# Hybrid mLSTM/attention encoder layer: the output projection's stores move from SP's queue to POOL's

## The chip, the cores and the metric

The kernel runs as one launch on one core of a Trainium2 chip. The metric is device time in microseconds (us), the median of several runs. The core's engines work through their own instruction queues, each in order: TensorE (PE, with a separate queue PEld for weight loads), VectorE (DVE), ScalarE (ACT), GpSimd (POOL) and SyncE (SP). Engines wait for one another through semaphores. A transfer (DMA) is issued by an instruction in the queue of one of the engines, and then runs by itself; in this kernel SP and POOL issue them.

## The reference

The reference is one encoder layer, in float32, over two groups of tokens with the same weights: 2048 prompt tokens and 256 sample tokens, 2304 in all, of width 1024.

```python
# per layer: x += W_out [ mLSTM_heads(n) ; GQA_heads(n) ],  n = RMSNorm(x)
#            x += W_down( silu(g) * a ),  [a; g] = DWConv3(W_up RMSNorm(x))
# final RMSNorm
D_MODEL = 1024; SEQ = 2048; DEC_SEQ = 256; D_FF = 2816
M_HEADS = 8; A_HEADS = 8; A_KV_HEADS = 2; HEAD_DIM = 64
```

A combined input projection feeds eight bidirectional mLSTM heads and eight query heads of attention, whose outputs are concatenated ("mix", width 1024). The output projection W_out brings mix back to the model's width and adds it to x; call the sum x1. A second RMSNorm of x1, call it n2, goes into the FFN: up projection, a width-3 depthwise convolution along the tokens, a gate, and the down projection, which is added to x1.

## The kernel before

Every float32 product is made on PE as three products of a shorter type, after a split of each operand into a high part (ACT) and the remainder, the low part (DVE). The phases are: input projections and norms; gates; then attention and mLSTM, interleaved; then the output projection, called phase_c, which starts while attention still has some query blocks to do and runs mixed with it; then the FFN, whose first loads and sums are mixed with the end of phase_c. All intermediate tensors go through DRAM: mix_d (the concatenated head outputs), x1_d (residual sums), n2_d (normalised rows), n2t_d (sums of n2 that a Strassen-like scheme for the up projection uses).

phase_c loads its weights first and splits them, and then goes through nine blocks of 256 tokens. For block b:

- `loads(b)`: eight loads from mix_d into the tiles cmx (L988), each split by ACT (L989) and DVE (L990), and eight loads of x into the four tiles cx{b}_0 to cx{b}_3 (L994). There are eight buffers for cx, so block b + 2 reuses those of block b.
- `mm(b, z)`: for each of four quarters z of the output columns, 48 matmuls into po (L1003); 9 × 4 × 48 = 1728 in all.
- `post(b, z)`: DVE adds po to cx in place (L1008); the sum is stored to x1_d (L1009, 128 partitions by 512 numbers, 256 KB); ACT squares it (L1011); POOL adds the squares up (L1013).
- `tail(b)`, called after the first quarter of the next block: POOL folds the sum of squares (L1016); a helper makes the reciprocal root mean square and broadcasts it to all partitions (PE L128, DVE L131, POOL L132, PE L134, tile rs_c); DVE multiplies cx in place by it and by the norm's weight, eight instructions (L1020); each quarter is stored to n2_d (L1022, 256 KB).

Before the change both stores go through `g.st`, which is `nc.sync`: SP's queue. POOL's own transfers near by are attention's stores into mix_d (L622), and earlier in the kernel the loads of k and v and, in mLSTM, those of dm (L821).

Attention, per block of queries: score products px and their maximum on DVE (L557, L558), a transpose of the maximum m4r (L566, PE L569 into pr), scores again (L580, L581), exponentials on ACT (L584, L585), the low part on DVE (pl, L586), products with v into pv (L598). At the end of a block ACT copies the sums out of pv (L606 the values, L607 the row sums), DVE takes reciprocals (L615, four instructions), POOL multiplies (L619) and issues two stores into mix_d (L622). Block b of phase_c can only start when the mix rows of its tokens are there; for the last block these come from attention's last query block.

The FFN's start: `n2_load` reads n2_d and n2t_d and splits (L1069 to L1071, tiles n and nt); `n2_sums` makes the sums (L1086 to L1092); `up_start` loads two slabs of the up weights (L1102, L1103, tiles ru), makes four weight sums on POOL (L1124 to L1127, tiles tw, one of them written over ru), splits (ACT L1115, DVE L1116) and multiplies into pa, pb, pc (L1119). The results go through ACT (L1135, L1206), the convolution on DVE (L1213) and the gate (L1287 to L1299). The down weights are loaded into rd (L1302), split into wd (ACT L1308, DVE L1309) and used at L1257; DVE adds into acc (L1259), which is first loaded from x1_d (L1189). The tiles ru, rd and rn share one pool of four buffers.

The order of instructions in each engine's queue is not the order of the program text. The framework simulates the timeline while it builds the program and puts out the instructions in the order in which they become ready in that simulation; attention's instructions have a higher priority. So an edit of one instruction's engine can change the order around it on all engines.

Of the kernel before, what the change touches and what calls it, by code (L numbers as in the profile page):

```python
# [36 lines left out]
BT = 256  # L37
# [48 lines left out]
def f32(ap):  # L86
    return ap.bitcast(F32)
# [14 lines left out]
def split(g, hi, lo, src, r, col=None):  # L102
    nc = g.nc
    nc.sync.dma_start(r, src)
    nc.scalar.activation(hi, r, AF.Copy, scale=1.0 if col is None else col)
    if col is None:
        nc.vector.tensor_tensor(lo, r, f32(hi), ALU.subtract)
    else:
        nc.vector.scalar_tensor_tensor(lo, r, col, f32(hi), ALU.mult, ALU.subtract)
# [10 lines left out]
def rstd_bc(g, sp, pp, sqs, n, ptag, name, bufs=1):  # L120


    nc = g.nc
    k = n // P
    ps = pp.tile([P, 512], F32, tag=ptag, name="rs_" + name, bufs=bufs)
    for t in range(k):
        for i, sq in enumerate(sqs):
            nc.tensor.matmul(ps[:, 504 + 2 * t:506 + 2 * t], sq[:, t * P:(t + 1) * P], g.ones, start=i == 0,  # L128
                             stop=i == len(sqs) - 1)
    r = sp.tile([P, 4], F32, tag="rcol", name="rcol_" + name)[:, 0:k]  # L130
    nc.vector.tensor_scalar(r, ps[:, 504:504 + 2 * k].rearrange("p (t o) -> p t o", o=2)[:, :, 0], EPS, None, ALU.add)  # L131
    nc.gpsimd.tensor_tensor(r, r, g.mhalf[:, 0:k], ALU.pow)  # L132
    for t in range(k):
        nc.tensor.matmul(ps[:, t * P:(t + 1) * P], r[:, t:t + 1].to_broadcast([P, P]), g.ident, start=True, stop=True)  # L134
    return ps[:, 0:n]
# [824 lines left out]
def phase_c(g, sn, sp, pp, wps):  # L960

    nc = g.nc
    wo = []
    g.normed = set()

    def weights(c):

        wo.append([wps[c // 4].tile([P, 2, 512], F32R, tag="w", name=f"wo{c}_{k}", bufs=WB) for k in range(2)])  # L970
        for k, w in enumerate(wo[c]):
            if c < 4:
                t = g.raw.tile([P, 512], F32, tag="raw", name=f"ro{c}_{k}", bufs=2)
            else:
                t = sp.tile([P, 512], F32, tag="x", name=f"ro{c}_{k}", bufs=CX)
            split(g, w[:, 0, :], w[:, 1, :], g.w_out[0, c * P:c * P + P, 512 * k:512 * k + 512], t)

    def loads(b):
        mx = []
        x = [sp.tile([P, 2, BT], F32, tag="x", name=f"cx{b}_{z}", bufs=CX) for z in range(4)]  # L980
        for z in range(4):
            for o in range(2):
                c = 2 * z + o
                if b % 2:
                    m = sp.tile([P, 2, BT], F32R, tag="mx", name=f"cmx{b}_{c}", bufs=MXB)
                else:
                    m = sn.tile([P, 2, BT], F32R, tag="nT", name=f"cmx{b}_{c}", bufs=NTB)
                nc.sync.dma_start(f32(m[:, 1]), g.mix_d[b, :, c])  # L988
                nc.scalar.activation(m[:, 0], f32(m[:, 1]), AF.Copy)  # L989
                nc.vector.tensor_tensor(m[:, 1], f32(m[:, 1]), f32(m[:, 0]), ALU.subtract)  # L990
                mx.append(m)
        for z in range(4):
            for t in range(2):
                nc.sync.dma_start(x[z][:, :, t * P:(t + 1) * P], g.xT[2 * b + t, :, 2 * z:2 * z + 2])  # L994
        return x, mx

    def mm(b, z, mx):
        po = pp.tile([P, 2, BT], F32, tag="po", name=f"po{b}_{z}")
        for o in range(2):
            n = slice(((2 * z + o) % 4) * P, ((2 * z + o) % 4 + 1) * P)  # L1000
            for c in range(NCC):
                for k, (a, h) in enumerate(((0, 0), (0, 1), (1, 0))):
                    nc.tensor.matmul(po[:, o], wo[c][z // 2][:, a, n], mx[c][:, h, :],  # L1003
                                     start=(c == 0 and k == 0), stop=(c == NCC - 1 and k == 2))
        return po

    def post(b, z, x, po, acc):
        nc.vector.tensor_tensor(x[z], po, x[z], ALU.add)  # L1008
        g.st.dma_start(g.x1_d[b, :, 2 * z:2 * z + 2], x[z])  # L1009
        q = acc if z == 0 else sp.tile([P, 2, BT], F32, tag="sq", name=f"csq{b}_{z}", bufs=1)  # L1010
        nc.scalar.activation(q, x[z], AF.Square, scale=1.0 / 32.0)  # L1011
        if z:
            nc.gpsimd.tensor_tensor(acc, acc, q, ALU.add)  # L1013

    def tail(b, x, acc):
        nc.gpsimd.tensor_tensor(acc[:, 0], acc[:, 0], acc[:, 1], ALU.add)  # L1016
        r = rstd_bc(g, sp, pp, [acc[:, 0]], BT, "r", f"c{b}")
        for z in range(4):
            for o in range(2):
                nc.vector.scalar_tensor_tensor(x[z][:, o], x[z][:, o], g.n2w[:, 2 * z + o:2 * z + o + 1],  # L1020
                                               r, ALU.mult, ALU.mult)
            g.st.dma_start(g.n2_d[:, 2 * z:2 * z + 2, b * BT:(b + 1) * BT], x[z])  # L1022
        g.normed.add(b)

    for c in range(NCC):
        weights(c)
        if c % WSTEP == WSTEP - 1:
            yield None
    prev = None
    for b in range(NB):  # L1030
        yield 2 * b
        x, mx = loads(b)
        for z in range(4):
            po = mm(b, z, mx)
            if z == 0:
                if prev is not None:
                    tail(*prev)
                acc = sp.tile([P, 2, BT], F32, tag="acc", name=f"cacc{b}", bufs=1)
            post(b, z, x, po, acc)
            if z < 3:  # L1040
                yield None
        prev = (b, x, acc)
    g.c_end = lambda: tail(*prev)


# [471 lines left out]
```

## Time and profile before

| | us |
|---|---|
| median of 3 runs | 3474.17 |
| lowest and highest | 3474.0, 3474.66 |
| the profiled execution's own time | 3475.05 |
| its span in the trace | 3473.3 |

The page of the profile lists 404.29 MB moved by DMA in 258,501 packets, 32.3% of the DMA engines' time for the transfers that SP and ACT issue ("hardware dynamic", q1) and 3.5% for those that POOL issues ("software dynamic", q0).

In a profile, L12 is line 12 of the kernel; "out<-in" are the names of tiles with buffer numbers left out. A row of the timeline gives the start, the length, the engine, the line and the operation, how many instructions were joined into the row ("x4"), and in brackets the idle time just before it and what released it. SPq and POOLq are the sequencers of SP and POOL: a DMA's issue is a row there, and the transfer itself a row "DMA". A row of the waits gives the engine and the line that waited, what it waited for, the total, the number of times and the longest.

### The profile page before, as it was taken

How to read it: one execution, taken by the hardware profiler on the slowest of the kernel's cores; microseconds unless marked ns; L12 is line 12 of the kernel's file. 1: busy time of each engine (PE TensorE's matmuls, PEld its weight loads, DVE VectorE, ACT ScalarE, POOL GpSimd, SP SyncE). 2: the span in 40 equal slices, each digit the busy share in tenths (PEclk: the TensorE clock that was granted, in tenths of full speed). 3: DMA queues.
4: the chain of work that ended last, by engine and by line, in shares of the span. 5: the costliest groups of instructions: out<-in, count | busy, mean ns of one | idle time of the engine just before them, and what ended most of it. 6: DMA issues, size and time to landing. Idle time of an engine off the chain costs nothing. (4 is left out here: it accounts for less than half of the span.)

```text
span 3473.3 us, 55765 instructions
## 1 busy us (share of the span) xinstructions
PE 3346.2 (96%) x20058; PEld 3103.0 (89%) x20058; DVE 2670.5 (77%) x4654; ACT 1930.9 (56%) x4329; POOL 1103.9 (32%) x1328
## 2 busy tenths in 40 slices
PE   7989999999999999999988999999999999999998
PEld 6878888888888887987778999999999998999998
DVE  6875687677777789767666888888888878887776
ACT  4536566666666766645554444446544446555555
POOL 6643133222224322211116233225333224322222
PEclk9999999999999999999999999999999999999999
DMA  6765334343355443432218233223333223421221
GB/s 222 238 197 162 117 107 118 104 131 101 105 169 161 131 144 115 145 105 70 68 51 296 73 97 98 74 65 130 127 105 99 67 73 119 145 65 63 73 73 50
DMA packets 258501, 404.29 MB, mean 116 GB/s; under 512 B 33552, under 2 KB 158256, under 8 KB 258224
## 3 DMA queue, kind: packets, MB, share of 16 engines
q1 hardware_dynamic: 230320, 358.24, 32.3%
q0 software_dynamic: 11344, 33.04, 3.5%
q10 hardware_dynamic: 16560, 9.44, 0.9%
q8 instruction: 158, 2.59, 0.3%
q14 instruction: 119, 0.97, 0.1%
HBM read 316.73 MB, written 83.90 MB: 115 GB/s over the span
## 5 line engine op out<-in xcount | busy, mean ns | idle before, releaser
L1257 PE MATMUL pd<-act,wd 128*128 128x384 f32 (+1 forms) x3120 | 593.2, 336 | 25.2 <-DVE acc L1259 14.4
L1257 PEld LDWEIGHTS pd<-act,wd 128*128 128x128 f32 x3120 | 539.5, 189 | 34.0 <-DVE acc L1259 20.0
L586 DVE TENSOR_TENSOR pl<-ps,ph 128x512 fp32r<-128x512 f32 x520 | 354.1, 685 | 235.3 <-ACT ps L585 228.2
L1119 PE MATMUL pa<-nt,wut 128*128 128x386 f32 (+2 forms) x2376 | 454.5, 339 | 2.0 <-DVE nt L1071 2.0
L1119 PEld LDWEIGHTS pa<-nt,wut 128*128 128x128 f32 x2376 | 421.4, 190 | 2.3 <-DVE nt L1071 2.3
L584 ACT ACTIVATE ph<-ps 128x512 fp32r<-128x512 f32 x520 | 309.7, 596 | 177.1 <-PE ps L581 172.3
L558 DVE TENSOR_REDUCE mx<-px 128x1 f32<-128x512 f32 (+1 forms) x528 | 343.8, 671 | 67.4 <-PE px L557 65.4
L1213 DVE SCALAR_TENSOR_TENSOR y<-u,cw,y 128x768 f32<-128x768 f32 (+1 forms) x264 | 314.0, 1190 | 36.3 <-ACT y L1206 29.2
L598 PE MATMUL pv<-ph,v 128*128 128x512 f32 (+1 forms) x1040 | 330.2, 405 | 2.9 <-ACT ph L584 2.4
L1124 POOL TENSOR_TENSOR tw<-ru 128x512 f32<-128x512 f32 x66 | 91.1, 1380 | 744.4 <-DMA ru<-w_up 573.3
L1135 ACT ACTIVATE u<-pa 128x386 f32<-128x386 f32 (+2 forms) x264 | 128.4, 486 | 328.4 <-PE pa L1119 326.9
L585 ACT ACTIVATE ps<-ps 128x512 f32<-128x512 f32 x520 | 310.9, 599 | 0.0
L1259 DVE TENSOR_TENSOR acc<-pd,acc 128x384 f32<-128x384 f32 (+1 forms) x544 | 280.6, 536 | 34.5 <-PE pd L1257 33.5
L1003 PEld LDWEIGHTS po<-cmx,wo 128*128 128x128 f32 x1728 | 233.9, 191 | 32.6 <-ACT cmx L989 16.2
L1003 PE MATMUL po<-cmx,wo 128*128 128x256 f32 x1728 | 242.2, 284 | 14.9 <-ACT cmx L989 14.8
L580 PE MATMUL ps<-qq,kk 128*128 128x512 f32 x520 | 217.0, 421 | 1.8 <-DVE pl L586 1.1
L557 PE MATMUL px<-kk,qq 128*128 128x512 f32 (+1 forms) x528 | 207.7, 411 | 6.6 <-DVE pl L586 3.5
L598 PE MATMUL pv<-pl,v 128*128 128x512 f32 x520 | 206.6, 407 | 6.9 <-DVE pl L586 6.6
L581 PE MATMUL ps<-qm,kl 65*128 65x512 f32 x520 | 209.1, 405 | 0.0
L724 PE MATMUL mj<-mn,wm 128*128 128x256 f32 x1296 | 197.4, 288 | 3.5 <-ACT og L738 2.1
L724 PEld LDWEIGHTS mj<-mn,wm 128*128 128x128 f32 x1296 | 182.1, 192 | 17.6 <-ACT og L738 2.5
L734 PE MATMUL mv<-wm,mn 128*128 128x256 f32 x1296 | 196.2, 288 | 1.1 <-ACT qb L730 0.9
(288 smaller groups left out, 7239.0 us busy)
## 6 DMA issues: line engine op xcount, KB each, us to landing
ru<-w_up SPq DMA_DIRECT2D x132, 512.0 KB, 3.4
mn<-n_d SPq DMA_DIRECT2D x216, 256.0 KB, 3.3
rd<-w_down SPq DMA_DIRECT2D x66, 512.0 KB, 3.6
n_d<-n1T SPq DMA_DIRECT2D x18, 1024.0 KB, 5.6
dm<-nm_d POOLq DMA_DIRECT2D x72, 256.0 KB, 4.0
mjn<-n_d SPq DMA_DIRECT2D x72, 256.0 KB, 3.3
mvn<-n_d SPq DMA_DIRECT2D x72, 256.0 KB, 3.2
q_d<-qz SPq DMA_DIRECT2D x18, 512.0 KB, 3.5
```

The lines of the kernel that those rows point to most:

```text
L558: nc.vector.tensor_reduce(s.mx[:, t, z0:z0 + 1], ps[:, 0:w], AX.X, ALU.max)
L580: nc.tensor.matmul(ps, kk[:, kc:kc + P], s.qq[:, 0:N], start=True, stop=False)
L584: nc.scalar.activation(ph, ps, AF.Exp)
L585: nc.scalar.activation(ps, ps, AF.Exp)
L586: nc.vector.tensor_tensor(pl, ps, f32(ph), ALU.subtract)
L598: nc.tensor.matmul(s.pv[0:HD if k in (1, 3) else P, 0:N], v, p, start=(kp == 0 and k == 0), stop=(2 * kp + 2 == s.nk and k == 5))
L724: nc.tensor.matmul(pj[:, o], s.w[c][:, a, o * P:(o + 1) * P], nT[c][:, :, h, :], start=(c + o + k == 0), stop=(c == NCC - 1 and k == 2 and ...
L1003: nc.tensor.matmul(po[:, o], wo[c][z // 2][:, a, n], mx[c][:, h, :], start=(c == 0 and k == 0), stop=(c == NCC - 1 and k == 2))
L1119: nc.tensor.matmul(p, w[:, aa, c, :], ops[k][:, c, bb, 0:n], start=c == 0 and i == 0 and not add, stop=c == NCC // 2 - 1 and i == 2, skip_ ...
L1213: nc.vector.scalar_tensor_tensor(y[:, s:e], u[:, s + k:e + k], cw[:, k, jj:jj + 1], y[:, s:e], ALU.mult, ALU.add)
L1257: nc.tensor.matmul(po, wds[j][c // 4][:, aa, c % 4 * P:(c % 4 + 1) * P], acts[j][:, bb, z0:z1], start=(j == 0 and k == 0), stop=(j == len( ...
L1259: nc.vector.tensor_tensor(accs[c][:, z0:z1], po, accs[c][:, z0:z1], ALU.add)
```

## The change

Two lines differ. In each, the issuing engine of a store is POOL instead of SP; the transfers are the same in source, target and size.

```diff
     def post(b, z, x, po, acc):
         nc.vector.tensor_tensor(x[z], po, x[z], ALU.add)
-        g.st.dma_start(g.x1_d[b, :, 2 * z:2 * z + 2], x[z])
+        nc.gpsimd.dma_start(g.x1_d[b, :, 2 * z:2 * z + 2], x[z])
...
                 nc.vector.scalar_tensor_tensor(x[z][:, o], x[z][:, o], g.n2w[:, 2 * z + o:2 * z + o + 1],
                                                r, ALU.mult, ALU.mult)
-            g.st.dma_start(g.n2_d[:, 2 * z:2 * z + 2, b * BT:(b + 1) * BT], x[z])
+            nc.gpsimd.dma_start(g.n2_d[:, 2 * z:2 * z + 2, b * BT:(b + 1) * BT], x[z])
```

They are executed 36 times each, nine blocks by four quarters. Other users of `g.st` keep SP.

## The prediction

> **What bounds the kernel now.** I read the page first: the span, busy shares, and the chain that ended last by engine.
>
> ```profile
> span 3473.3 us, 55765 instructions
> PE 3346.2 (96%) x20058; PEld 3103.0 (89%) x20058; DVE 2670.5 (77%) x4654; ACT 1930.9 (56%) x4329; POOL 1103.9 (32%) x1328
> PE 34%; DVE 7%; DMA 3%; issue 1%; ACT 1%; POOL 0%; SPq 0%; POOLq 0%; DVEq 0%; ACTq 0%
> ```
>
> PE is busy for 96% of the span. SP's and POOL's queues have 0% of the chain of waits, so an issue slot is not in itself what ends the program. PE's 127 us of idle time are spread over everything; the question is how much lies where the diff acts. The 72 stores fall between 1409.7 and 1892.0 us, so the second view is the table of windows over 1388 to 1912 us (columns: length, then busy time and count for PE, weight loads, DVE, ACT, POOL, then granted clock, DMA share, GB/s).
>
> ```profile
> ...
> 1560.00:1640.00 80.00, 73.66 (x402) 59.77 (x402) 53.92 (x93) 43.09 (x84) 11.09 (x13) 0.96 0.21 63
> 1640.00:1720.00 80.00, 74.60 (x409) 59.38 (x408) 55.73 (x96) 43.51 (x84) 10.16 (x11) 0.98 0.20 60
> 1720.00:1800.00 80.00, 74.63 (x384) 59.87 (x383) 54.24 (x94) 46.95 (x93) 8.08 (x9) 0.94 0.19 56
> ...
> 1815.00:1829.00 14.00, 0.08 (x1) 0.00 (x0) 6.40 (x13) 1.60 (x3) 2.39 (x3) 0.66 0.66 189
> 1829.00:1872.00 43.00, 42.98 (x346) 42.98 (x347) 20.89 (x29) 12.88 (x20) 32.12 (x30) 0.95 0.95 324
> 1872.00:1912.00 40.00, 36.02 (x198) 35.36 (x198) 34.03 (x43) 26.41 (x46) 24.07 (x15) 0.96 0.81 273
> sum 524.00, PE 488.00 PEld 424.67 DVE 354.80 ACT 276.47 POOL 123.22; mean PE 48.80 PEld 42.47 DVE 35.48 ACT 27.65 POOL 12.32
> ```
>
> In these 524 us PE is idle for 36: 17.1 in the three 80 us windows (6.34 + 5.40 + 5.37), 13.9 in the gap from 1815 to 1829, 4.0 after 1872, 1 elsewhere. That 36 us (1.0% of the span) caps any gain. The view of waits over 1380 to 1960 us says who ends them (total, times, longest).
>
> ```profile
> SPq L1009 <- DVE cx L1008: 94.4, 21, 11.6
> SPq L1022 <- DVE cx L1020: 65.8, 24, 16.5
> POOL o L619 <- DVE rs L615: 131.0, 9, 29.5
> ...
> PE po L1003 <- ACT cmx L989: 14.8, 3, 13.9
> PE pv L598 <- DVE pl L586: 6.5, 5, 1.8
> PE pr L569 <- DVE m4r L566: 6.0, 3, 4.1
> ```
>
> SP does stand behind the stores: 94.4 + 65.8 us of its queue is waiting for DVE's results, with loads behind. But PE's own waits are for DVE (attention's maximum m4r, its low half pl) and once, for 13.9 us, for cmx. None but the cmx wait ends in a load.
>
> **The change part by part.** It takes 36 stores of x1 (L1009) and 36 of n2 (L1022) off SP's queue and issues the same 72 transfers, 256 KB each, on POOL. Nothing is computed differently. What a slot costs on either queue is in the views by source line.
>
> ```profile
> L1009 SPq DMA_DIRECT2D x_d<-cx x36: 319/326/865, 1409.7 to 1874.9; - x36
> DMA to landing us min/median/max: 2.1/2.6/6.0
> L1022 SPq DMA_DIRECT2D n_d<-cx x36: 359/371/1139, 1459.4 to 1892.0; - x36
> L622 POOL DMA_DIRECT2D mix_d<-o x56: 532/577/714, 284.3 to 1823.7; - x56
> DMA to landing us min/median/max: 1.9/2.6/7.7
> L821 POOL DMA_DIRECT2D dm<-nm_d x72 | 43.2, 600 | 47.4 <-PE mN L866 24.3 <-PE px L557 17.9 <-PE pv L598 3.1
> ```
>
> SP is relieved of 36 × 0.326 + 36 × 0.371 = 25 us of issuing. POOL takes on 72 × 0.58 to 0.60 = 42 to 43 us, from the two groups that it issues now; with 123.2 us of work it would stand at 166 of 524 us, 32%. The landing is the same for both issuers in the median (2.6 us), at most 7.7 against 6.0 us. The Trainium skill, "DMA: Bandwidth & Descriptors", section on issuing engines, says the same engines carry a DMA whoever issues it and that changing the issuer saves only the usually small time of the initiation; taken alone it would make the sum 0. The rows agree as far as landing goes.
>
> **In the steady blocks** (1440 to 1800 us) I let POOL's changed order run against the times of before. Its only op there with someone waiting is attention's L619, and that waits for DVE L615 itself, up to 29.5 us; the four n2 stores of a block fall into that wait. An x1 store gets between L619 and its mix store L622 in two blocks, 0.6 us on a store that nobody needs for many microseconds. New waits: DVE L1020 overwrites in place the tile that the x1 store reads, so it now waits for a landing on POOL's queue. The next fence has one such pair: store issued on SP at 1798.82, overwritten from 1814.89, slack 16 us against a landing of at most 7.7. Behind L1020 stand attention's in-order DVE ops (L586, L558, L566), so a late landing would hold attention; I take 0. If POOL issued every x1 store as late as the slack allows, each further microsecond would cost DVE one, so the bound is open above; below, freed loads could save part of the 17.1 us. What PE waits for there is DVE, and DVE's sum ahead of each maximum is the same in the changed order, so I take 0 of these.
>
> **The gap before 1829.** Attention's last block ends, its mix rows are stored, and the last output block needs them.
>
> ```profile
> 1798.82 0.38 SPq L1009 DMA_DIRECT2D x_d<-cx  x1
> ...
> 1808.29 0.40 PE L598 MATMUL pv<-ph,v 128*64 128x512 f32 x1
> 1808.53 0.39 PE L598 MATMUL pv<-pl,v 128*128 128x512 f32 x1
> ...
> 1814.24 0.60 PE L134 MATMUL rs_c<-ident,rcol_c 128*128 128x128 f32 x4
> 1814.60 0.48 PE L598 MATMUL pv<-pl,v 128*128 128x512 f32 x1
> 1829.02 29.12 PE L1003 MATMUL po<-cmx,wo 128*128 128x256 f32 x228 [13.93 <-ACT cmx L989]
> ...
> 1814.89 3.22 DVE L1020 SCALAR_TENSOR_TENSOR cx<-cx,nw,rs_c 128x256 f32<-128x256 f32 x8 [3.25 <-PE rs_c L134]
> 1818.03 3.37 DVE L615 RECIPROCAL rs<-rs 64x128 f32<-64x128 f32 x4
> ...
> 1815.74 0.59 ACT L607 ACTIVATE rs<-pv 64x512 f32<-64x512 f32 x1
> ...
> 1821.53 1.25 POOL L619 TENSOR_TENSOR o<-o,rs 64x512 f32<-64x512 f32 x1 [10.00 <-DVE rs L615]
> 1823.08 1.14 POOL L622 DMA_DIRECT2D mix_d<-o  x2 [0.29 <-POOL o L619]
> ```
>
> Eight L1020 (3.22 us) run on DVE ahead of the reciprocal L615, though its input is ready at 1815.74 + 0.59 = 1816.33; it starts at 1818.03, 2.95 us after the last pv (1814.60 + 0.48 = 1815.08). In the changed order the broadcast L134 stands earlier: behind it come 6 po and 4 pv, 6 × 0.128 (29.12/228) + 4 × 0.24 (the two pv starts) = 1.7 us, of which I count 1.6. L1020 then starts 1.6 us before the last pv ends and is done 3.22 − 1.6 = 1.6 us after it. L615 starts there: 2.95 − 1.6 = 1.3 us gained. Five po matmuls also move behind the last pv, into the gap: 5 × 0.128 = 0.6. Sum −1.9 us. POOL now issues four n2 stores ahead of L619, the last at 1.6 us after pv, done at 2.2; L619 can start at 1.6 + 3.4 = 5.0. L615 hides them; if not, 4 × 0.6 = 2.4 us would come on top.
>
> **The transition to the FFN** (1855 to 1912 us). POOL does the weight sums L1124 to L1127 there and is already 32.12 of 43 us busy; six or seven stores, 3.6 to 4.2 us, fall on it.
>
> ```profile
> 1863.31 1.29 POOL L1127 TENSOR_TENSOR tw<-ru,tw 128x512 f32<-128x512 f32 x1
> ...
> 1864.56 1.30 POOL L1013 TENSOR_TENSOR cacc<-cacc,csq 128x512 f32<-128x512 f32 x1
> ...
> 1864.68 0.61 SPq L1302 DMA_DIRECT2D rd<-w_down  x1
> ...
> 1864.68 6.44 DMA rd<-w_down
> ...
> 1882.92 1.16 PE L1119 MATMUL pa<-nt,wut 128*128 128x386 f32 x5 [1.98 <-DVE nt L1071]
> ...
> 1905.61 2.04 PE L1119 MATMUL pa<-n,wu 128*128 128x386 f32 x10 [2.01 <-DVE wu L1116]
> ...
> 1904.87 0.68 DVE L1116 TENSOR_TENSOR wu<-ru,wu 128x512 fp32r<-128x512 f32 x1
> ```
>
> In the changed order one x1 store and one L1013 come ahead of L1127, whose buffer the load of rd needs: the load issues at 1864.6 + 1.3 + 0.6 = 1866.5, 1.9 us late. The same stretch loses 1 MB of n2 stores just ahead of that load, which took 6.44 us to land; the landing can come back by as much. I take 0 between +1.9 and −1.9. One matmul group of the first FFN columns comes to follow one more DVE split L1116 than now (0.68): +0.7, bounds 0 and two of them, 1.4. The stall of 2.01 us probably goes, as the DVE split L1116 stands ahead of two convolution steps that it follows now; but those steps then come late for the down projection, so I take half, −1.0, bounds −2.0 and 0. After it the order is the same as before.
>
> Sum: −1.9 + 0 + 0.7 − 1.0 = −2.2 us. The profiled execution took 3475.05 us (1.75 around the span), so 3472.85; its excess over the median of runs, 3474.17, is 0.88, so **3472.0 us**.
>
> **The rivals.** **(1) SP was the bottleneck**: with loads ahead of all stores the scheduler's reorder takes both transition stalls (4.0), the gap's 1.9 and a third of the 17.1 in the steady blocks (5.7), 11.6 in all: 3462.6 us. For it: 160 us of SP's waiting. Against it: the waits that PE has in the blocks end with DVE.
>
> **(2) POOL becomes the bound (slower)**: its in-order queue holds an x1 store behind tensor work or behind a wait for L615 (up to 29.5 us), the landing comes after L1020's turn, and DVE stands still with attention behind it. It decides once issue plus landing passes the slack of about 16 us. Each of the last four blocks could lose 29.5 + 2.6 − 16 = 16 us at worst; a quarter of it in each makes 16, and with the gap's −1.9 the time is 3474.2 + 14.1 = 3488.3 us. Against it: in the changed order the x1 stores stand behind that wait only when their own data is later still.
>
> **(3) The transfers were hidden anyway**, and the reorders cancel: 3474.2 us. It shares the forecast's side of the bound.
>
> **(4) DVE holds POOL's issuing up.** If a POOL issue had to wait for the DVE op that runs, the four n2 stores would come after the gap's L615 and add their 4 × 0.6 = 2.4 us, and the seven stores of the transition would each wait for an op like L1116, 7 × 0.68 = 4.8: 3472.0 + 7.2 = 3479.2 us. Against it: L622's longest issue, 0.714 us, is only 0.14 over its median on a DVE that is busy two thirds of the time. The Trainium skill, "SBUF — State Buffer", section on the two separate sides, tells of such a lock-out of descriptor writes while DVE runs, at some 620 against 3100 ns. By that figure, an estimate, the gap's four stores alone would take 12.4 us, 9 more than L615 hides; L622's row disagrees with it.
>
> **How the numbers follow.** Forecast and (3) together 0.46; rival (1) 0.27; rival (2) 0.23; rival (4) 0.04. A measurement of this kernel tells about 0.2% (6.9 us) from no change, so faster is 0.27 (rival 1), slower 0.23 (rival 2), the same 0.50 (the rest). The range goes down to (1), 3462, and up to 3483, two thirds of the way to (2), since a smaller lateness is likelier than a large one; some 0.2 lies outside. The forecast's own range, from its bounds, is 3468.4 (−1.9 − 1.9 − 2.0) to 3478.0 (−1.9 + 2.4 + 1.9 + 1.4).
>
> **What would show it.** Right: SP's waits at L1009 and L1022 gone; the gap 12.0 us with L615 starting 1.6 us after the last pv; the three 80 us windows still at 5 to 6 us of idle PE; the stall of 2.01 gone or halved. Wrong: DVE waiting at L1020 for a store's landing, POOL issues longer than 0.71 us, L619 started later than its L615, or the blocks' idle time falling well below 5 us, which would mean that loads did bound them.

## The result: slower by 0.25%

The changed kernel takes 3481.3 us in the median of ten runs (3474.89 to 3487.67), the kernel before 3472.82 us in ten (3470.73 to 3474.66). The ratio is 1.0025 with a 95% interval of 1.0015 to 1.0034: about 8 us lost. A second set of runs gave 1.0022 (1.0013 to 1.0030). The time lies inside the predicted range, but the forecast was 3472.0 us, a gain of 2.2; no change was the likeliest case and a gain the next. The profiled execution of the changed kernel took 3478.35 us (span 3476.6), one of its shorter runs, against 3475.05 us before.

A line of the page, and the same windows as before (length, then busy time and count of PE, weight loads, DVE, ACT, POOL, then granted clock, DMA share, GB/s), of the changed kernel:

```profile
PE 3350.1 (96%) x20058; PEld 3104.4 (89%) x20058; DVE 2677.8 (77%) x4654; ACT 1930.8 (56%) x4329; POOL 1149.4 (33%) x1400
...
1560.00:1640.00 80.00, 73.60 (x395) 59.41 (x394) 54.37 (x92) 43.27 (x84) 15.38 (x19) 0.94 0.21 63
1640.00:1720.00 80.00, 75.04 (x396) 60.31 (x395) 55.00 (x95) 43.47 (x84) 14.71 (x18) 0.91 0.19 59
1720.00:1800.00 80.00, 74.24 (x383) 59.65 (x382) 53.47 (x91) 44.84 (x87) 13.82 (x19) 0.94 0.17 52
...
1872.00:1912.00 40.00, 36.31 (x194) 34.29 (x193) 35.86 (x39) 20.74 (x37) 32.72 (x26) 0.91 0.65 218
```

POOL has taken the 72 issues on (1328 to 1400 instructions, 1103.9 to 1149.4 us). The idle time of PE in the three steady windows is 6.40 + 4.96 + 5.76 = 17.1 us, as before: nothing was won there and nothing lost. The waits over 1380 to 1960 us show who stands where now:

```profile
POOL x_d L1009 <- DVE cx L1008: 150.6, 27, 22.6
POOL o L619 <- DVE rs L615: 124.5, 11, 24.5
POOL n_d L1022 <- DVE cx L1020: 21.7, 8, 5.7
...
PE pc L1119 <- ACT u L1135: 5.7, 1, 5.7
```

The waiting for DVE has moved from SP's queue into POOL's (150.6 + 21.7 us), and a new wait of PE stands out, the last row: a matmul of the up projection, pc, waits 5.7 us for a copy out of a bank on ACT. To place the loss I compare the start of the same matmul in both traces. The rows below, one kernel after the other, are the views of L1003 and of L1257; the first and last start stand at the end of a row.

```profile
L1003 PE MATMUL po<-cmx,wo x1728: 275/282/582, 1388.5 to 1872.4; 128*128 128x256 f32 x192
L1257 PE MATMUL pd<-act,wd x3120: 276/337/522, 1922.0 to 3437.2; 128*128 128x384 f32 x186, 128*128 128x256 f32 x9
...
L1003 PE MATMUL po<-cmx,wo x1728: 274/282/583, 1387.9 to 1873.9; 128*128 128x256 f32 x192
L1257 PE MATMUL pd<-act,wd x3120: 276/337/685, 1932.4 to 3441.1; 128*128 128x384 f32 x186, 128*128 128x256 f32 x9
```

From the first to the last po the changed kernel takes 486.0 us against 483.9, about 2 us more. From the last po to the first matmul of the down projection, the same 248 matmuls in both kernels, it takes 58.4 us against 49.6: 8.8 us more. After that the order of work is the same, and in this execution the rest is 6.5 us shorter, some of it because PE's waits at L1257 fall from 25.2 to 21.0 us. The medians differ by more than these two executions do, so that much given back is not typical. The loss lies in one stretch of 60 us, the start of the FFN. The rows of the changed kernel there, by engine:

```profile
1867.16 1.30 POOL L1127 TENSOR_TENSOR tw<-ru,tw 128x512 f32<-128x512 f32 x1
...
1882.30 1.74 POOL L1013 TENSOR_TENSOR cacc<-cacc,csq 128x512 f32<-128x512 f32 x1
1884.01 1.72 POOL L1127 TENSOR_TENSOR tw<-ru,tw 128x512 f32<-128x512 f32 x1
1885.69 2.27 POOL L1071 TENSOR_TENSOR nt<-nt 128x772 fp32r<-128x772 f32 x1
1887.92 1.18 POOL L1016 TENSOR_TENSOR cacc<-cacc 128x256 f32<-128x256 f32 x1
...
1904.94 3.05 POOL L1022 DMA_DIRECT2D n_d<-cx  x4
...
1876.25 4.57 DVE L1309 TENSOR_TENSOR wd<-rd,wd 128x512 fp32r<-128x512 f32 x2 [1.28 <-ACT wd L1308]
1903.75 3.21 DVE L1020 SCALAR_TENSOR_TENSOR cx<-cx,nw,rs_c 128x256 f32<-128x256 f32 x8
...
1910.70 0.63 ACT L1115 ACTIVATE wut<-tw 128x512 fp32r<-128x512 f32 x1 [1.78 <-PE pa L1119]
1911.24 1.93 ACT L1206 ACTIVATE y<-u,cw 128x768 f32<-128x768 f32 x2
1912.92 3.87 DVE L1213 SCALAR_TENSOR_TENSOR y<-u,cw,y 128x767 f32<-128x767 f32 x3
1916.82 0.84 ACT L1287 ACTIVATE y<-y 128x768 f32<-128x768 f32 x1 [1.83 <-DVE y L1213]
...
1918.10 3.80 PE L1119 MATMUL pc<-n,wu 128*128 128x386 f32 x12 [5.66 <-ACT u L1135]
```

and those of the kernel before for the same instructions:

```profile
1875.67 1.29 POOL L1013 TENSOR_TENSOR cacc<-cacc,csq 128x512 f32<-128x512 f32 x1 [1.95 <-ACT csq L1011]
1877.04 1.07 POOL L1016 TENSOR_TENSOR cacc<-cacc 128x256 f32<-128x256 f32 x1
...
1888.76 3.22 DVE L1020 SCALAR_TENSOR_TENSOR cx<-cx,nw,rs_c 128x256 f32<-128x256 f32 x8 [2.12 <-PE rs_c L134]
1889.65 2.71 SPq L1022 DMA_DIRECT2D n_d<-cx  x4
1896.30 1.95 ACT L1206 ACTIVATE y<-u,cw 128x768 f32<-128x768 f32 x2
1904.98 0.85 ACT L1287 ACTIVATE y<-y 128x768 f32<-128x768 f32 x1 [2.26 <-DVE y L1213]
```

Read the changed rows from the end. PE's pc needs a bank that ACT's L1135 has to empty. On ACT, L1135 stands behind the silu L1287, which waits for the convolution L1213 on DVE, which follows L1206 at 1911.24 (before: 1896.30). L1206 writes the tile y, and experiments 6, 10 and 12 show that its tile is free only when the second of block 8's four n2 stores has landed: there L1206 waits for them and starts 0.1 to 0.2 us after the second. These stores begin at 1904.94 (before: 1889.65), after L1020 at 1903.75 (before: 1888.76), and that comes after L1016, which runs on POOL at 1887.92 instead of 1877.04. From L1016 on every step is 11 to 15 us late.

Two things make L1016 late. On POOL it now stands behind a weight sum and an operand split (L1127, L1071), 4.0 us together. The other 6.6 us are there already at the last L1013 of the block (1882.30, before 1875.67): DVE's last L1008 comes at 1880.74 instead of 1874.19, behind the two L1309.

Two things also hold y itself. The second store is issued at 1905.7 and lands 3.2 us later, at 1908.9; before, it landed at 1892.6 (1890.4 + 2.2). So y cannot start before 1908.9, which is 12.6 of its 14.9 us of lateness. The last 2.3 us are the order on ACT: splits of the next up weights (L1115) stand ahead of y, and the last of them waits 1.78 us for PE. The chain that ended last in this trace runs through that split, the convolution, the silu and L1135 to the pc, not through the store.

PE's waiting explains 5.4 of the 8.8 us, since the waits of PE in the stretch add up to 9.4 us (four of them) where they were 4.0 (1.98 + 2.01). The other 3.4 us are slower matmuls: over the stretch (1873.95 to 1932.36 us, before 1872.40 to 1922.00) PE is busy for 49.05 us instead of 45.62, and the granted clock is 0.88 instead of 0.97. The twelve pc behind the wait take 3.80 us, where twelve of L1119 took 2.27 to 2.30 before; the granted clock from 1918 to 1922 us is 0.59.

### The profile page after: what moved, and what is told of

Same layout as the page of the kernel before. It is cut to its first block, busy times and chain, and to the rows that moved or that the text cites. A ratio compares the mean times of both kernels' runs of the same rounds, so it can differ in the third digit from the quotient of the medians.

```text
span 3476.6 us, 55865 instructions
## 1 busy us (share of the span) xinstructions
PE 3350.1 (96%) x20058; PEld 3104.4 (89%) x20058; DVE 2677.8 (77%) x4654; ACT 1930.8 (56%) x4329; POOL 1149.4 (33%) x1400
## 5 line engine op out<-in xcount | busy, mean ns | idle before, releaser
L1257 PE MATMUL pd<-act,wd 128*128 128x384 f32 (+1 forms) x3120 | 593.0, 336 | 21.0 <-DVE acc L1259 12.3
L1257 PEld LDWEIGHTS pd<-act,wd 128*128 128x128 f32 x3120 | 540.1, 189 | 29.7 <-DVE acc L1259 17.9
L1119 PE MATMUL pa<-nt,wut 128*128 128x386 f32 (+2 forms) x2376 | 455.0, 339 | 0.5 <-DVE nt L1071 0.5
L1119 PEld LDWEIGHTS pa<-nt,wut 128*128 128x128 f32 x2376 | 421.3, 190 | 1.5 <-DVE nt L1071 1.0
L1213 DVE SCALAR_TENSOR_TENSOR y<-u,cw,y 128x768 f32<-128x768 f32 (+1 forms) x264 | 310.7, 1178 | 36.9 <-ACT y L1206 29.9
L1135 ACT ACTIVATE u<-pa 128x386 f32<-128x386 f32 (+2 forms) x264 | 128.4, 486 | 319.5 <-PE pa L1119 319.3
L1003 PEld LDWEIGHTS po<-cmx,wo 128*128 128x128 f32 x1728 | 233.2, 192 | 30.5 <-ACT cmx L989 14.2
L1003 PE MATMUL po<-cmx,wo 128*128 128x256 f32 x1728 | 242.2, 284 | 13.4 <-ACT cmx L989 13.2
L724 PEld LDWEIGHTS mj<-mn,wm 128*128 128x128 f32 x1296 | 182.1, 192 | 17.1 <-ACT og L738 2.5
```

What stands on the lines that cost most here:

```text
L724: nc.tensor.matmul(pj[:, o], s.w[c][:, a, o * P:(o + 1) * P], nT[c][:, :, h, :], start=(c + o + k == 0), stop=(c == NCC - 1 and k == 2 and ...
L1119: nc.tensor.matmul(p, w[:, aa, c, :], ops[k][:, c, bb, 0:n], start=c == 0 and i == 0 and not add, stop=c == NCC // 2 - 1 and i == 2, skip_ ...
L1213: nc.vector.scalar_tensor_tensor(y[:, s:e], u[:, s + k:e + k], cw[:, k, jj:jj + 1], y[:, s:e], ALU.mult, ALU.add)
L1257: nc.tensor.matmul(po, wds[j][c // 4][:, aa, c % 4 * P:(c % 4 + 1) * P], acts[j][:, bb, z0:z1], start=(j == 0 and k == 0), stop=(j == len( ...
```

## The experiments

Thirteen runs follow; 3 is the changed kernel once more, the others are kernels of their own. "Stretch" is the time from the last po to the first matmul of the down projection in the one profiled execution of each. Before: 49.6 us, block 8's L1020 at 1888.8, first L1206 at 1896.3.

| | stores on POOL | ratio to before (95%) | stretch | L1020 of block 8 | first L1206 |
|---|---|---|---|---|---|
| changed | all 72 | 1.0025 (1.0015–1.0034) | 58.4 | 1903.8 | 1911.2 |
| 1 | blocks 0 to 6 | 0.9996 (0.9987–1.0005) | 53.2 | 1889.9 | 1897.5 |
| 2 | blocks 7, 8 | 1.0038 (1.0025–1.0050) | 60.1 | 1904.3 | 1912.6 |
| 3 | all, repeated | 1.0022 (1.0013–1.0030) | 58.4 | 1900.2 | 1907.6 |
| 4 | all n2 | 1.0022 (1.0013–1.0031) | 56.9 | 1906.0 | 1913.3 |
| 5 | all, norm first | 1.0017 (1.0009–1.0026) | 55.3 | 1893.1 | 1908.7 |
| 6 | all but n2 of 8 | 1.0010 (1.0002–1.0019) | 56.3 | 1899.1 | 1904.4 |
| 7 | n2 of 8 | 1.0005 (0.9997–1.0014) | 51.0 | 1890.6 | 1901.5 |
| 8 | all x1 | 0.9996 (0.9987–1.0004) | 52.2 | 1893.0 | 1900.4 |
| 9 | all but n2 of 7 | 1.0001 (0.9992–1.0010) | 53.6 | 1893.0 | 1900.4 |
| 10 | n2 of 7 | 1.0003 (0.9994–1.0011) | 49.7 | 1899.5 | 1903.5 |
| 11 | all but n2 of 7, 8 | 0.9996 (0.9987–1.0004) | 52.4 | 1891.7 | 1899.1 |
| 12 | all, convolution first | 1.0032 (1.0019–1.0044) | 59.1 | 1902.5 | 1910.7 |
| 13 | n2 of 7, 8 | 1.0021 (1.0011–1.0031) | 56.5 | 1899.4 | 1906.5 |

### 1 and 2: which blocks

In both stores the issuing engine depends on the block; 2 has `b >= 7` in the same place.

```diff
-        nc.gpsimd.dma_start(g.x1_d[b, :, 2 * z:2 * z + 2], x[z])
+        (nc.gpsimd if b < 7 else g.st).dma_start(g.x1_d[b, :, 2 * z:2 * z + 2], x[z])
...
-            nc.gpsimd.dma_start(g.n2_d[:, 2 * z:2 * z + 2, b * BT:(b + 1) * BT], x[z])
+            (nc.gpsimd if b < 7 else g.st).dma_start(g.n2_d[:, 2 * z:2 * z + 2, b * BT:(b + 1) * BT], x[z])
```

> Both stores go to POOL for blocks 0 to 6 only; blocks 7 and 8 keep SP. Theory T (the loss lies at the transition to the FFN: POOL's in-order queue puts stores that wait for DVE ahead of the weight sums L1124 to L1127, and these come late): 3471 to 3476 us, the first down matmul (L1257) at 1920 to 1925 us, as before (1922.0), not 1932.4 as in the changed kernel. Theory B (the loss lies in the steady blocks, stores beside attention): 3479 to 3483 us.

> Both stores go to POOL for blocks 7 and 8 only, 16 of 72 transfers. T: 3478 to 3483 us with the first down matmul near 1930 us or later. B: 3471 to 3476 us, first down matmul near 1922.

Measured: 3470.86 us against 3470.98, ratio 0.9996, first down matmul at 1923.4; and 3484.37 us, 1.0038, first down matmul at 1933.9. Both times lie just outside T's ranges, by 0.1 us below and 1.4 us above, and far from B's. The 56 stores of blocks 0 to 6 cost nothing and bring nothing that can be told; the 16 stores of the last two blocks carry the whole loss. Theory T holds as to the place, B falls.

### 3: the changed kernel once more

> The changed kernel once more, for a second profile. T: the first down matmul again within 2 us of 1932.4, and what differs between executions (3474.9 to 3487.7 us so far) is gained or lost after it. If the loss is chance, the first down matmul comes at 1922 to 1928 in this execution.

3478.62 us, 1.0022. The first down matmul came at 1929.2, 3.2 us from the other profile and not within 2, but all of this execution is earlier, and the stretch is 58.4 us again, with the same wait:

```profile
1914.49 4.19 PE L1119 MATMUL pc<-n,wu 128*128 128x386 f32 x12 [5.66 <-ACT u L1135]
```

This execution took 3474.98 us in all, its FFN behind the stretch being 6.6 us shorter than before's, as in the first profile. So the loss at the FFN's start is not chance; what is given back later varies.

### 4 and 8: which of the two stores

Each undoes one of the diff's two lines: in 4 the x1 store goes back to SP, in 8 the n2 store.

```diff
-        nc.gpsimd.dma_start(g.x1_d[b, :, 2 * z:2 * z + 2], x[z])
+        g.st.dma_start(g.x1_d[b, :, 2 * z:2 * z + 2], x[z])
```

> Only the 36 normalised-row stores (L1022) go to POOL; the 36 x1 stores (L1009) stay on SP. If the x1 stores that wait for DVE L1008 ahead of the sum L1127 are the cause within T: 3471 to 3476 us, L1127 done near 1864.6, first down matmul 1920 to 1925. If the n2 stores do it as well: 3477 to 3482 us and a first down matmul after 1927.

> Only the 36 x1 stores go to POOL. POOL's order keeps the sum of squares L1016 of block 8 ahead of L1127 and L1071, as before. M: 3471 to 3477 us, first down matmul 1922 to 1927, L1020 of block 8 within 4 us of its time before (1888.8). Q: 3477 to 3482 us.

Only n2: 3477.94 us, 1.0022, first down matmul at 1935.3 (last po at 1878.4), and a wait of 5.70 us on L1135. Only x1: 3472.75 us, 0.9996, first down matmul at 1924.2, L1020 of block 8 at 1893.0, 4.3 us later than before. The x1 stores are innocent; the n2 stores do it. My suspicion in 4, an x1 store ahead of L1127, was wrong.

### 5: block 8's norm ahead of POOL's operand splits

All stores on POOL; L1071 on POOL is held until the reciprocal root of block 8 (L132) is issued. Later lines move by one.

```diff
-    nc.gpsimd.tensor_tensor(r, r, g.mhalf[:, 0:k], ALU.pow)
+    g.powc = nc.gpsimd.tensor_tensor(r, r, g.mhalf[:, 0:k], ALU.pow).ins
...
-        getattr(nc, engs[z // 2]).tensor_tensor(lo, f32(lo), f32(hi), ALU.subtract)
+        with g.tc.issue_after(g.powc) if b == 0 and k in LATE and engs[z // 2] == G else nullcontext():
+            getattr(nc, engs[z // 2]).tensor_tensor(lo, f32(lo), f32(hi), ALU.subtract)
```

> All 72 stores on POOL as in the changed kernel, but POOL's four operand splits L1071 of the FFN are put behind the reciprocal root of block 8 (L132), so that L1020 of block 8 and its four stores come earlier. Theory M (the FFN's tiles y stand in the memory that block 8's tiles cx give free when their n2 stores have landed; the late stores of block 8 make the convolution late, silu blocks ACT, and PE waits 5.7 us for a bank): the stall of 5.7 us goes or falls below 2.5 us, the conv step L1206 starts near 1902 instead of 1911, the first down matmul at 1923 to 1927, 3471 to 3476 us. Rival Q (the lateness is POOL's queue as a whole, weight sums and operand splits behind 3 us of stores): the first down matmul stays after 1929, 3478 to 3483 us.

3479.34 us, 1.0017. L1020 came at 1893.13 and the wait on the copy shrank as M says, but other waits took its place, and the first down matmul came at 1928.1:

```profile
1883.47 2.30 PE L1120 MATMUL pc<-nt,wut 128*128 128x386 f32 x6 [3.07 <-DVE nt L1072]
...
1915.20 2.41 PE L1120 MATMUL pc<-n,wu 128*128 128x386 f32 x12 [1.14 <-ACT u L1136]
...
1898.81 2.92 POOL L1022 DMA_DIRECT2D n_d<-cx  x4
```

The four stores still stand behind POOL's splits, at 1898.81, and y (its L1206 is L1207 here) was begun only at 1908.7. The edit moves the lateness more than it removes it. M is half borne out: its time was missed by 3.3 us, and 3479.34 lies in the range of the rival Q.

### 6, 7, 9, 10, 11 and 13: four stores at a time

Blocks 7 and 8 have four n2 stores each. Here every combination is tried, once in the changed kernel and once in the kernel before. As an example the edit of 9; the others change the condition or, in 7, 10 and 13, start from the kernel before.

```diff
-            nc.gpsimd.dma_start(g.n2_d[:, 2 * z:2 * z + 2, b * BT:(b + 1) * BT], x[z])
+            (g.st if b == 7 else nc.gpsimd).dma_start(g.n2_d[:, 2 * z:2 * z + 2, b * BT:(b + 1) * BT], x[z])
```

> The changed kernel with the four n2 stores of block 8 alone back on SP; L1020 of block 8 stays as late as in the changed kernel (near 1904). If the late L1020 is what makes y late: 3476 to 3481 us, PE's stall of 5.7 us shrinks by the 1.5 us that POOL's slower issuing costs, at most by 3. If POOL's issue of these four stores were the cause by itself: 3470 to 3475 us, no stall over 2.5 us.

> The kernel before with the four n2 stores of block 8 alone on POOL; L1020 of block 8 stays early (near 1889), and the four stores stand ahead of the sums L1124 of the next column. M: 3471 to 3476 us with the first down matmul at 1922 to 1926, since the stores still land by about 1898. If any late store of block 8 on POOL is enough: 3477 to 3482 us.

> The changed kernel with the four n2 stores of block 7 alone back on SP; 68 stores stay on POOL, block 8's among them. Theory N (block 7's four stores, which wait on POOL for DVE's L1020 in the midst of the weight sums, push the sum of squares L1016 of block 8 behind POOL's operand splits; from there the norm of block 8, its stores and the FFN's y tiles are late): 3471 to 3476 us, L1020 of block 8 near 1892 instead of 1903.75, first down matmul 1923 to 1927. Rival Q (the 3 us of block 8's stores on POOL and its load as a whole): 3478 to 3483 us, first down matmul after 1929.

> The kernel before with the four n2 stores of block 7 alone on POOL, 4 of 72. N: most of the loss is there: 3476 to 3481 us, L1020 of block 8 after 1900, first down matmul after 1927 and a PE wait on ACT L1135 of over 3 us. Q: 3470 to 3474 us, as before.

> The changed kernel with the n2 stores of blocks 7 and 8 on SP; all x1 stores and the n2 stores of blocks 0 to 6 on POOL, 64 of 72. N: 3470 to 3474 us, as before, or at most 3 us less if the freed loads in the blocks bring anything; first down matmul 1922 to 1926. Q (POOL's load by x1 stores at the transition counts too): 3475 to 3480 us.

> The kernel before with the n2 stores of blocks 7 and 8, eight of 72, on POOL. Each four alone cost nothing that could be told (1.0003 and 1.0005). Theory S (their delays add on one chain, and only the sum passes the slack ahead of PE's wait for L1135): L1020 of block 8 after 1900, y (L1206) after 1909, a wait of PE on ACT L1135 of 4 to 6.5 us, 3476 to 3482 us. Rival (the n2 stores of blocks 0 to 6 carry the loss): 3470 to 3475 us, no such wait.

In 6 the time was 3477.34 us and the wait on L1135 3.6 us, as expected of the late L1020. In 7 the time was 3474.86 us and the first down matmul came at 1923.2, as M says. In 9 (3474.01 us, L1020 at 1893.0, first down matmul at 1926.6) and in 11 (3471.99 us, 1922.9) N was right and Q wrong.

The ratios, ordered by where the two groups of four are issued:

| | 7 on SP, 8 on SP | 7 on SP, 8 on POOL | 7 on POOL, 8 on SP | both on POOL |
|---|---|---|---|---|
| all other stores on SP | 1 (before) | 1.0005 | 1.0003 | 1.0021 |
| all other stores on POOL | 0.9996 | 1.0001 | 1.0010 | 1.0025 (changed) |

Eight of the 72 stores make the loss, and neither four alone has a loss that can be told with the rest on SP. With the rest on POOL, block 7's four alone have a small one (1.0010). Both fours together lose more than the sum of the two in either row, but only by 0.0013 and 0.0010, where each interval is ±0.0009 or more; the ratios alone do not settle it, and the traces have to speak. N, which put it all on block 7, missed in 10: L1020 was late as expected (1899.5), but the time was 3473.62 us and not 3476 to 3481; it is the rival's. The pair 10 and 13 shows why; they differ in the issuer of block 8's four stores alone. The rows of 10:

```profile
1903.48 1.95 ACT L1206 ACTIVATE y<-u,cw 128x768 f32<-128x768 f32 x2 [1.70 <-DMA n_d<-cx]
1907.99 0.84 ACT L1287 ACTIVATE y<-y 128x768 f32<-128x768 f32 x1
1909.27 2.39 PE L1119 MATMUL pc<-n,wu 128*128 128x386 f32 x12 [1.14 <-ACT u L1135]
```

and of 13:

```profile
1900.88 2.91 POOL L1022 DMA_DIRECT2D n_d<-cx  x4
1905.97 0.63 ACT L1115 ACTIVATE wut<-tw 128x512 fp32r<-128x512 f32 x1 [2.17 <-PE pa L1119]
1906.50 1.93 ACT L1206 ACTIVATE y<-u,cw 128x768 f32<-128x768 f32 x2
1912.48 0.84 ACT L1287 ACTIVATE y<-y 128x768 f32<-128x768 f32 x1 [2.22 <-DVE y L1213]
1913.76 4.22 PE L1119 MATMUL pc<-n,wu 128*128 128x386 f32 x12 [5.71 <-ACT u L1135]
```

L1020 comes at the same time (1899.5 and 1899.4), but with POOL's issue y starts 3.0 us later, the silu 4.5 us later, and PE's wait grows from 1.14 to 5.71 us. Of the 3.0 us, 1.0 is the landing: the second store lands at 1903.4 in 10 (1901.2 + 2.2) and at 1904.4 in 13 (1901.6 + 2.8). The other 2 us are the order on ACT: in 13 two splits L1115 stand ahead of y, the last after a wait of 2.17 us for PE; in 10 they come behind it. In the silu's 4.5 us there is also the convolution, whose first three L1213 take 4.89 us in 13 and 2.87 in 10. Only the issuer of four stores differs, so it acts in two ways: by the landing, and by the order of instructions that the framework's simulation makes of it. In 10 the lateness of L1020 alone costs PE 1.14 us at this place; block 7 has used up the slack, and what block 8's stores add arrives at PE almost whole.

In 9 it is the other way round: L1020 is early (1893.0), block 8's stores are on POOL, y starts at 1900.4, and the pc does not wait on L1135. Theory S holds for the time (3480.28 us) and the wait; it expected L1020 after 1900 and L1206 after 1909, both too late.

### 12: the convolution ahead of the next splits

All stores on POOL; the splits of the up weights of columns 24 and 25 are held behind the convolution of columns 22 and 23. Lines behind move by one to three.

```diff
-                    nc.vector.scalar_tensor_tensor(y[:, s:e], u[:, s + k:e + k], cw[:, k, jj:jj + 1], y[:, s:e],
+                    yi = nc.vector.scalar_tensor_tensor(y[:, s:e], u[:, s + k:e + k], cw[:, k, jj:jj + 1], y[:, s:e],
                                                    ALU.mult, ALU.add)
+                    if b == 0 and (jj, k) == (NFC + 1, 2):
+                        g.y0 = yi.ins
...
-        nc.scalar.activation(hi, src, AF.Copy)
-        nc.vector.tensor_tensor(lo, src, f32(hi), ALU.subtract)
+        with g.tc.issue_after(g.y0) if b == 0 and jj == NFC + 2 else nullcontext():
+            nc.scalar.activation(hi, src, AF.Copy)
+            nc.vector.tensor_tensor(lo, src, f32(hi), ALU.subtract)
```

> All 72 stores on POOL, but the splits of the up weights for columns 24 and 25 (ACT L1115, DVE L1116) are put behind the convolution of columns 22 and 23, so that y (L1206, here L1207) no longer stands behind splits that wait for PE. Theory M (y's tile waits for the landing of block 8's n2 stores on POOL): ACT waits ahead of L1207 for a landing, L1207 starts at 1908 or later, and the first down matmul comes no earlier than 1929; 3477 to 3484 us. Theory O (only the order of instructions holds y back, the tile is free in time): L1207 starts at 1903 to 1907, PE's wait of 5.7 us falls below 3, first down matmul before 1929; 3473 to 3478 us.

3484.51 us, 1.0032, 0.5 us above M's range; first down matmul at 1930.0. The first row is L1206 under its new number; below it stand the four n2 stores:

```profile
1910.67 1.94 ACT L1207 ACTIVATE y<-u,cw 128x768 f32<-128x768 f32 x2 [3.02 <-DMA n_d<-cx]
...
L1022 POOL DMA_DIRECT2D n_d<-cx x4: 725/730/752, 1903.7 to 1906.0; - x4
DMA to landing us min/median/max: 5.9/6.1/6.2
```

With the splits out of its way, ACT stands ready for y and waits 3.02 us for the landing of an n2 store. The tile y lies in the memory of cx tiles of block 8 and is free only when their stores have landed: the second store, issued at 1904.4, lands 6.1 us later, and y starts at 1910.67. PE's wait on the copy is 8.4 us. In 10 the same wait is 1.70 us, in 6 0.25 us. That part of M is shown, and O's times are all missed.

But 12 does not tell how much the release alone costs in the changed kernel. Its stores took 6.1 us to land, where they took 3.2 there; SP issued the eight loads of acc (L1189, here L1190) from 1902.97, ahead of the stores, and in the changed kernel from 1908.62, behind them. In the changed kernel the tile was free at 1908.9, and ACT's order held y for 2.3 us more. What PE would lose by either of the two alone no run shows.

## Why the prediction failed, point by point

**The place of the bound, right.** SP's waiting, 160 us, was no bound: with it gone the three steady windows have the same 17.1 us of PE idle time, and experiments 1 and 11 are at 0.9996. Rival (1), a gain of 11.6 us, has nothing behind it.

**The steady blocks, right.** Nothing there waits for POOL: the landing of an x1 store did not hold L1020, and L619 kept its wait for L615. Rival (2) named the right resource, POOL's in-order queue, but the wrong place and tile.

**The gap, right in mechanism.** L615 starts at 1818.22, 1.5 us after the last pv (1.6 forecast), and POOL's four n2 stores end before L619:

```profile
1816.30 0.39 PE L598 MATMUL pv<-pl,v 128*128 128x512 f32 x1
1816.25 3.08 POOL L1022 DMA_DIRECT2D n_d<-cx  x4 [5.66 <-DVE cx L1020]
1818.22 3.37 DVE L615 RECIPROCAL rs<-rs 64x128 f32<-64x128 f32 x4
1821.75 1.25 POOL L619 TENSOR_TENSOR o<-o,rs 64x512 f32<-64x512 f32 x1 [2.42 <-DVE rs L615]
...
1830.46 2.75 PE L1003 MATMUL po<-cmx,wo 128*128 128x256 f32 x11 [13.17 <-ACT cmx L989]
```

The gap is 13.2 us against 13.9; in this execution the way from L619 to the first po, with its two transfers, took 8.7 us (1830.46 − 1821.75) against 7.5 before (1829.02 − 1821.53), and that ate the rest. In the eight other executions with the x1 stores of blocks 0 to 6 on POOL the same row has a gap of 12.2 to 12.5 us, and in the five with those on SP 13.8 to 14.9. So the term of −1.9 is nearer −1.5. It did not shorten the phase: from the first po to the last, the nine executions with them on POOL take 483.2 to 486.0 us, the kernel before 483.9.

**The transition, wrong.** The forecast there was −0.3 us (0 + 0.7 − 1.0); it was +8.8. For the 0.7 there is a row of its kind: pb waits 1.02 us for L1116 at 1894.17. The step that failed is this one: "The stall of 2.01 us probably goes, as the DVE split L1116 stands ahead of two convolution steps that it follows now; but those steps then come late for the down projection, so I take half". The stall did go, and the convolution did come late, but the first to feel it was not the down projection: ACT's in-order queue passed the lateness through the silu to the copy L1135, and so to PE, which waited 5.66 us there. In place of −1.0 stand 5.4 us more of waiting and 3.4 us of slower matmuls, for which the sum had no term.

The lateness has its origin in what I put at nothing. Among the new waits I named only DVE's L1020, which overwrites the tile of the x1 store; I did not follow how late block 8's norm would be, nor who gets the memory of block 8's tiles next. That is the FFN's y, and to it the four last n2 stores are no tail that nobody waits for, but the release of a buffer. It came at 1908.9 instead of 1892.6.

**The signs and the number.** Most signs listed for a right forecast came true (no waits of SP at the stores, the 80 us windows, the stall), and the sum was wrong all the same, since the wait that mattered was on neither list. Of the signs against it one came true: POOL's issue of an n2 store takes 0.725 to 0.776 us, above 0.71. That is no waiting for DVE as in rival (4), for the median, 0.728, is hardly above the least. That 3481.3 us lies in the range is luck: the range was drawn up to 3483 for the sake of rival (2), whose loss lay in the steady blocks, and the forecast's own bounds end at 3478.0.

**The rd chain, right for the load and not followed further.** L1127 ended at 1868.46, 3.9 us late and not 1.9, and the load of rd was issued at 1868.48. But it landed in 3.4 us instead of 6.4, and so at 1871.9, only 0.8 us later than before: the landing did come back, as the forecast allowed. What it left out stands behind: ACT's L1308 had to wait in its queue for L1011 (1875.06), which waited for DVE's L1008, and L1309 began 4.4 us late and took 4.57 us instead of 2.39. By itself this chain cost little: in experiment 8 the load of rd comes at 1871.8, later still, and the stretch is 52.2 us.

**The landing.** I took it as equal for both issuers, from L622, whose transfers are 64 and 128 KB. For the x1 stores it was, 2.6 us in the median on both. For the n2 stores it was not: 3.2 us in the median of all 36, against 2.3 on SP. Block 8's, of the changed kernel and below it of the kernel before:

```profile
L1022 POOL DMA_DIRECT2D n_d<-cx x4: 725/728/752, 1904.9 to 1907.3; - x4
DMA to landing us min/median/max: 3.1/3.2/4.2
...
L1022 SPq DMA_DIRECT2D n_d<-cx x4: 359/368/378, 1889.7 to 1892.0; - x4
DMA to landing us min/median/max: 2.2/2.2/2.4
```

Issue and landing are slower by 0.36 and 1.0 us. The landing is not the issuer's alone: in experiment 6 the same four stores took 3.3 to 3.6 us from SP. And the landing alone is not the 3.0 us between experiments 10 and 13, two thirds of which are ACT's order.

**What stays open.** What the late landing and ACT's order would each cost alone. Why experiment 2 is slower than the changed kernel and than 13, if it is (the intervals overlap). How much of the lateness the FFN gives back in an average run: 1 and 9 have stretches 3.6 and 4.0 us longer than before and no loss, and 6 and 13 nearly the same stretch (56.3 and 56.5 us) at 1.0010 and 1.0021, so one execution's stretch is no measure of the median. No combination was clearly faster than the kernel before.

## What to carry to other kernels

A store is the release of its tile. Before moving a phase's last stores to another queue, find out which tile takes that memory in the next phase, and treat the landing as an input of its first user. And where a queue with little work is filled up, look at the few microseconds in which it is busy rather than at its mean: POOL, busy for 32% of the 524 us from 1388 to 1912, was busy for 32.72 of the 40 us from 1872 to 1912, in which the loss begins. Two delays that cost little alone can add on one chain, so a two-by-two of the halves says more than undoing one of them.

## What the runs showed of the hardware

A split on DVE can be held up by tensor work on POOL. Of the two L1309 at 1876.25, which take 4.57 us together, one takes 3.97 us and the other 0.68. Beside the first, POOL ran L1013, L1125 and L1126 one behind the other until 1879.65. Two more L1309 of the same shape, at 1896.00, took 1.28 us together; POOL then ran only the small L132 (128 by 2 numbers).

```profile
1875.85 1.30 POOL L1013 TENSOR_TENSOR cacc<-cacc,csq 128x512 f32<-128x512 f32 x1
...
1878.36 1.29 POOL L1126 TENSOR_TENSOR ru<-ru,ru 128x512 f32<-128x512 f32 x1
...
1896.00 1.28 DVE L1309 TENSOR_TENSOR wd<-rd,wd 128x512 fp32r<-128x512 f32 x2
```

The Trainium skill, "SBUF — State Buffer", section on who interferes with whom, says that a DVE instruction with both inputs in SBUF contends with POOL instructions that read SBUF. These rows agree: the 3.3 us that the one split takes longer are about the 3.4 us that POOL's three still had to run, and these kept their usual 1.3 us each. So an edit that only shifts POOL's work in time can lengthen DVE's.
